# Lower parts of the first feed-forward weights by an adding DMA, and matmuls grouped by width

## The chip, the cores and the metric

The kernel runs on one core of one Trainium2 chip. The metric is the device time of one execution in microseconds (us). Before the change it is 2393.61 us, the median of 3 runs (2393.53 to 2394.68).

## The reference

Two transformer blocks, one after the other, on 256 tokens of width 2048 in float32. The first block has a modulated norm, a mixer of dilated attention and a gated recurrence, and a feed-forward part; the second has stick-breaking attention and a feed-forward part. The change lies in the two feed-forward parts, which are alike:

```python
# first block
h2 = rms_norm(x, norm2_w[l]) * (1.0 + scale2) + shift2
ff = jnp.square(jax.nn.relu(h2.astype(dt) @ w_ff1[l])) @ w_ff2[l]
x = x + (gate2 * ff.astype(jnp.float32)).astype(dt)
# second block
def squared_relu_mlp(h, w_in, w_out):
    return jnp.square(jax.nn.relu(h @ w_in)) @ w_out
h = h + squared_relu_mlp(rms_norm_2(h, norm_mlp_g[i]), mlp_w_in[i], mlp_w_out[i])
```

`w_ff1` and `mlp_w_in` are 2048 x 8192, `w_ff2` and `mlp_w_out` 8192 x 2048. All weights are read once, from HBM.

## The kernel before

TensorE works on a rounded 32-bit type (`F32R`) here, so each float32 operand is held as two: `hi`, its rounded value, and `lo`, what rounding left out. A product is the sum of three matmuls: hi by hi, hi by lo, lo by hi.

Weights come in chunks of 256 rows by 512 columns (512 KB). `chunk` (L222) makes one: SP's queue loads `raw`, ACT copies it to `hi` (L230), DVE subtracts `hi` from `raw` into `lo` (L231). There are 7 buffers of `raw` (RAW), shared with the loads of the modulation weights `w_ada`, and 4 each of `hi` and `lo` (HL). Both operations have a raised priority (AHEAD), so the scheduler, which fixes the order of every engine when the program is built, puts them well ahead of the matmuls that use the chunk.

Three functions consume chunks. `gemm` (L237) has the weights as the moving operand, 512 wide, 12 matmuls for a chunk. `gemm_t` (L250) has them as the stationary operand, with 24 matmuls of 256 columns. `gemm_wide` (L265), the one the change touches, also has the weights stationary, and for each of its 8 pairs in a chunk issues one matmul of 512 columns with `hi` (the upper and lower parts of the activations side by side, L275) and one of 256 columns with `lo` (the upper part alone, L276). Its four accumulators are two banks of `psA` (`acc`) and two of `psB` (`ps`).

`ffn` (L847) is called once for each block. For each quarter of the hidden width it runs four blocks of 8 chunks into `hT` (a wide phase: 32 chunks of `w_ff1` or `mlp_w_in`), then 32 chunks of `gemm` with the second weights. Only in the first quarter of the first call are two of the four blocks done by `gemm_t`. So `gemm_wide` runs 30 times, on 240 chunks, in seven phases of 32 chunks and one of 16. After each block ACT copies four pieces out of the accumulators (L866), DVE adds the other halves (L867) and squares (L868), ACT rounds the result (L869) and DVE subtracts (L870).

During the first `ffn`, `tick` also issues one load of `w_ada` (512 KB) for every four chunks (L916), until these 32 loads are done. POOL does a few memsets only, and issues no DMA.

Of the kernel before, what the change touches and what calls it, by code (L numbers as in the profile page):

```python
# [10 lines left out]
F32 = mybir.dt.float32  # L11
# [3 lines left out]
AF = mybir.ActivationFunctionType  # L15
ALU = mybir.AluOpType
AX = mybir.AxisListType

P = 128
T = 256  # L20
D = 2048
NK = D // P
# [3 lines left out]
KC = 2  # L26
# [14 lines left out]
def kernel(ctx: ExitStack, tc: tile.TileContext, I: dict, out: bass.AP, dbg=None):  # L41
    nc = tc.nc
    V, S, G, TE = nc.vector, nc.scalar, nc.gpsimd, nc.tensor
# [156 lines left out]
    def step(queue):  # L200
        while queue:
            try:
                next(queue[0])
                return
            except StopIteration:
                queue.pop(0)
# [4 lines left out]
    def tick():  # L211
        for name, queue in (("ada", ada_queue), ("side", side_queue)):
            due[name] += rate[name]
            while due[name] >= 1.0:
                due[name] -= 1.0
                step(queue)
# [2 lines left out]
        while queue:  # L219
            step(queue)  # L220

    def chunk(w, r0, c0):  # L222
        raw = wp.tile([P, KC, 512], F32, tag="raw", name="raw", bufs=RAW)
        nc.sync.dma_start(
            out=raw, in_=w[r0 : r0 + KC * P, c0 : c0 + 512].rearrange("(j p) n -> p j n", p=P)
        )
        hi = wp.tile([P, KC, 512], F32R, tag="hi", name="hi")
        lo = wp.tile([P, KC, 512], F32R, tag="lo", name="lo")
        with tc.high_priority(offset=AHEAD):
            S.copy(hi, raw)  # L230
            V.tensor_tensor(lo, raw, hi.bitcast(F32), ALU.subtract)  # L231
        return hi, lo

    def banks2():
        return [psA.tile([P, 512], F32, tag="acc", name="acc") for _ in range(2)]

    def gemm(xh, xl, both, w, r0, c0, accs, kr=(0, NK), first=True, last=True):  # L237

        for k0 in range(kr[0], kr[1], KC):
            hi, lo = chunk(w, r0 + k0 * P, c0)  # L240
            for t in range(2):
                for j in range(KC):
                    k = k0 + j
                    a, b = xh[:, k, t * P : (t + 1) * P], xl[:, k, t * P : (t + 1) * P]
                    TE.matmul(accs[t], a, hi[:, j, :], start=first and k == kr[0], stop=False)  # L245
                    TE.matmul(accs[t], a, lo[:, j, :], start=False, stop=False)  # L246
                    TE.matmul(accs[t], b, hi[:, j, :], start=False, stop=last and k == kr[1] - 1)  # L247
            tick()

    def gemm_t(xh, xl, both, w, r0, c0, accs, kr=(0, NK), first=True, last=True):  # L250

        for k0 in range(kr[0], kr[1], KC):
            hi, lo = chunk(w, r0 + k0 * P, c0)
            for m in range(4):
                o = accs[m // 2][:, (m % 2) * T : (m % 2 + 1) * T]
                for j in range(KC):
                    k = k0 + j
                    a, b = hi[:, j, m * P : (m + 1) * P], lo[:, j, m * P : (m + 1) * P]

                    TE.matmul(o, a, xh[:, k, :], start=first and k == kr[0] and m % 2 == 0, stop=False, skip_group_check=True)  # L260
                    TE.matmul(o, a, xl[:, k, :], start=False, stop=False, skip_group_check=True)  # L261
                    TE.matmul(o, b, xh[:, k, :], start=False, stop=last and k == kr[1] - 1, skip_group_check=True)  # L262
            tick()

    def gemm_wide(xh, xl, both, w, r0, c0, accs):  # L265

        for k0 in range(0, NK, KC):
            hi, lo = chunk(w, r0 + k0 * P, c0)  # L270
            for m in range(4):
                for j in range(KC):
                    k = k0 + j
                    a, b = hi[:, j, m * P : (m + 1) * P], lo[:, j, m * P : (m + 1) * P]
                    TE.matmul(accs[m], a, both[:, k, :, :], start=k == 0, stop=False, skip_group_check=True)  # L275
                    TE.matmul(accs[m][:, T : 2 * T], b, xh[:, k, :], start=False, stop=k == NK - 1,  # L276
                              skip_group_check=True)
            tick()

    def transposes(dst, src):  # L280
# [202 lines left out]
    for g, kr in enumerate(GROUPS[:-1]):  # L483
        while len(ready) <= g:
            ada_tick()
        for f, c0 in early:
            accs = banks2()
# [18 lines left out]
    ang, m, n, tmp, na = (sp.tile([P, 32], F32, tag="rope", name="rope", bufs=5) for _ in range(5))  # L506
# [314 lines left out]
    for b in range(4):  # L821
        accs = banks2()
# [24 lines left out]
    def ffn(xT, w1, w2, done, halfway=None):  # L847
        facc = None
        for c in range(4):
# [7 lines left out]
            for b in range(4):  # L857
                if b < len(pend):
                    accs = pend[b]
                    gemm_t(*xT, w1, 0, b * 512, accs, kr=(8, 16), first=False)  # L860
                else:
                    accs = banks2() + [bank(), bank()]
                    gemm_wide(*xT, w1, 0, c * D + b * 512, accs)
                    r = big().rearrange("p (a b) -> p a b", a=4)
                    for m in range(4):
                        S.copy(r[:, m, :], accs[m][:, T : 2 * T])  # L866
                        V.tensor_tensor(r[:, m, :], r[:, m, :], accs[m][:, 0:T], ALU.add)  # L867
                    V.scalar_tensor_tensor(r, r, 0.0, r, ALU.max, ALU.mult)  # L868
                    S.copy(hT[0][:, 4 * b : 4 * b + 4, :], r)  # L869
                    V.tensor_tensor(hT[1][:, 4 * b : 4 * b + 4, :], r, hT[0][:, 4 * b : 4 * b + 4, :].bitcast(F32),  # L870
                                    ALU.subtract)
                    continue
                for i in range(2):
                    k = b * 4 + i * 2
                    r = big()[:, 0:512].rearrange("p (a b) -> p a b", a=2)
                    S.activation(r, accs[i].rearrange("p (a b) -> p a b", a=2), AF.Relu)
                    V.tensor_tensor(r, r, r, ALU.mult)
                    S.copy(hT[0][:, k : k + 2, :], r)
                    V.tensor_tensor(hT[1][:, k : k + 2, :], r, hT[0][:, k : k + 2, :].bitcast(F32), ALU.subtract)
# [110 lines left out]
    for b in range(4):  # L990
# [4 lines left out]
        if b in pend:  # L995
            accs = pend.pop(b)
            gemm(*oT, wo, 0, b * 512, accs, kr=(12, 16), first=False)
        else:
            accs = banks2()
# [83 lines left out]
```

## Time and profile before

| | |
|---|---|
| median of 3 runs | 2393.61 us |
| the profiled execution | 2398.15 us, of which the span from first to last instruction is 2396.4 us |
| TensorE busy | 97% of the span, mean granted clock 0.993 |
| VectorE, ScalarE, GpSimd busy | 65%, 49%, 0% |
| HBM read | 514.95 MB, mean 216 GB/s over the span |

PE is TensorE, PEld its weight loads, DVE VectorE, ACT ScalarE, POOL GpSimd, SP SyncE, which here issues nearly all loads. Matmuls are pipelined: the duration of one (0.28 or 0.40 us) is longer than the distance from its start to the next one's start, and it is this distance that counts. A few per cent of the matmul records can be missing from a trace. Idle time of an engine that bounds nothing costs nothing. A group's releaser, after the arrow, is what ended most of its waiting.

### The profile page before, as it was taken

The numbers are of one execution on the slowest core, as the hardware profiler recorded it, in microseconds if no ns is written. First come the engines' busy times: TensorE is split into PE (matmuls) and PEld (weight loads), VectorE is DVE, ScalarE is ACT, GpSimd is POOL, SyncE is SP. The second block draws the span as 40 slices with busy tenths as digits, with TensorE's granted clock in tenths as the row PEclk, the third lists the DMA queues.
The fourth block names the chain that finished last, engine by engine and source line by source line (L and its number), as shares of the span: only waits on it lengthen the run. The fifth ranks groups of instructions, "written<-read, shape, count | busy, mean of one in ns | idle before, by whom it ended". The sixth has DMA issues, their size and how long they took to land.

```text
span 2396.4 us, 31309 instructions
## 1 busy us (share of the span) xinstructions
PE 2334.1 (97%) x11951; PEld 1972.5 (82%) x11951; DVE 1554.5 (65%) x1871; ACT 1174.2 (49%) x1749; POOL 5.9 (0%) x10
## 2 busy tenths in 40 slices
PE   5999999998999999999999999999999999999999
PEld 4887888877988888888888888888888888888887
DVE  7899888878665665555566555565654554555564
ACT  4535575644444444444445566655544443443442
POOL 0000000000000000000000000000000000000000
PEclk9999999998999999999999999999999999999999
DMA  9998787887777776666656555555666666666663
GB/s 347 333 318 272 260 293 248 271 294 274 229 239 235 231 237 211 186 192 189 188 185 186 178 169 163 162 171 177 187 191 194 187 190 194 185 191 194 186 196 129
DMA packets 252312, 519.10 MB, mean 217 GB/s; under 512 B 16689, under 2 KB 17278, under 8 KB 251906
## 3 DMA queue, kind: packets, MB, share of 16 engines
q1 hardware_dynamic: 252010, 517.03, 67.6%
q8 instruction: 93, 1.52, 0.3%
q14 instruction: 57, 0.47, 0.1%
q10 hardware_dynamic: 152, 0.08, 0.0%
HBM read 514.95 MB, written 2.10 MB: 216 GB/s over the span
## 4 chain that ended last, share of the span: by engine, by line
PE 88%; DVE 6%; issue 3%; DMA 2%; ACT 1%; SPq 0%; DVEq 0%; ACTq 0%
PE acc L246 16%; PE acc L247 16%; PE acc L245 16%; PE ps L275 9%; PE acc L275 9%; PE acc L276 5%; PE ps L276 5%; DVE lo L231 2%; PE acc L262 2%; PE ps L281 2%; PE acc L261 2%; PE acc L260 2%; DMA raw<-in_w_ada_dram 1%; PE ps L641 1%; DVE w L447 1%
## 5 line engine op out<-in xcount | busy, mean ns | idle before, releaser
L231 DVE TENSOR_TENSOR lo<-raw,hi 128x1024 fp32r<-128x1024 f32 x784 | 958.5, 1223 | 740.4 <-ACT hi L230 738.3
L230 ACT CAST hi<-raw 128x1024 fp32r<-128x1024 f32 x784 | 823.3, 1052 | 1026.4 <-PE acc L247 576.2
L245 PE MATMUL acc<-hi,yT 128*128 128x512 f32 x1280 | 501.0, 391 | 0.0
L246 PE MATMUL acc<-lo,yT 128*128 128x512 f32 x1280 | 499.7, 390 | 0.0
L247 PE MATMUL acc<-hi,yT 128*128 128x512 f32 x1280 | 499.5, 390 | 0.0
L275 PE MATMUL acc<-xT,hi 128*128 128x512 f32 x960 | 350.1, 399 | 0.0
L275 PE MATMUL ps<-xT,hi 128*128 128x512 f32 x960 | 349.2, 398 | 0.0
L246 PE MATMUL acc<-lo,xT 128*128 128x512 f32 x704 | 279.6, 397 | 4.2 <-DVE lo L231 3.6
L247 PEld LDWEIGHTS acc<-hi,yT 128*128 128x128 f32 x1280 | 241.0, 188 | 50.1
L245 PEld LDWEIGHTS acc<-hi,yT 128*128 128x128 f32 x1280 | 240.9, 188 | 49.7
L246 PEld LDWEIGHTS acc<-lo,yT 128*128 128x128 f32 x1280 | 241.0, 188 | 49.2
L247 PE MATMUL acc<-hi,xT 128*128 128x512 f32 x704 | 276.7, 393 | 0.0
L245 PE MATMUL acc<-hi,xT 128*128 128x512 f32 x704 | 276.0, 398 | 0.0
L276 PE MATMUL acc<-xT,lo 128*128 128x256 f32 x960 | 269.6, 281 | 0.0
L276 PE MATMUL ps<-xT,lo 128*128 128x256 f32 x960 | 269.5, 281 | 0.0
L275 PEld LDWEIGHTS acc<-xT,hi 128*128 128x128 f32 x960 | 180.3, 188 | 44.4 <-ACT hi L230 0.5
L275 PEld LDWEIGHTS ps<-xT,hi 128*128 128x128 f32 x960 | 180.3, 188 | 44.3
L140 DVE SCALAR_TENSOR_TENSOR ada<-raw,csil,ada 128x1024 f32<-128x1024 f32 x124 | 158.6, 1280 | 43.2 <-DMA raw<-in_w_ada_dram 42.6
L276 PEld LDWEIGHTS acc<-xT,lo 128*128 128x128 f32 x960 | 181.4, 189 | 0.8 <-issue 0.5
L276 PEld LDWEIGHTS ps<-xT,lo 128*128 128x128 f32 x960 | 181.4, 189 | 0.0
L246 PEld LDWEIGHTS acc<-lo,xT 128*128 128x128 f32 x704 | 132.9, 189 | 36.9 <-DVE lo L231 10.8
L247 PEld LDWEIGHTS acc<-hi,xT 128*128 128x128 f32 x704 | 132.8, 189 | 26.8 <-issue 0.2
(226 smaller groups left out, 1935.2 us busy)
## 6 DMA issues: line engine op xcount, KB each, us to landing
raw<-in_w_ff_dram SPq DMA_DIRECT2D x256, 512.0 KB, 4.0
raw<-in_w_ada_dram SPq DMA_DIRECT2D x160, 512.0 KB, 4.8
raw<-in_mlp_w_in_dram SPq DMA_DIRECT2D x128, 512.0 KB, 3.7
raw<-in_mlp_w_out_dram SPq DMA_DIRECT2D x128, 512.0 KB, 3.7
raw<-in_w_in_dram SPq DMA_DIRECT2D x112, 512.0 KB, 5.8
raw<-in_sb_w_qkv_dram SPq DMA_DIRECT2D x96, 512.0 KB, 3.9
ada<-in_w_ada_dram SPq DMA_DIRECT2D x32, 512.0 KB
raw<-in_w_out_dram SPq DMA_DIRECT2D x32, 512.0 KB, 5.5
```

Source lines behind the costliest of these rows:

```text
L140: V.scalar_tensor_tensor(acc, w, csil[:, k : k + 1], acc, ALU.mult, ALU.add)
L230: S.copy(hi, raw)
L231: V.tensor_tensor(lo, raw, hi.bitcast(F32), ALU.subtract)
L245: TE.matmul(accs[t], a, hi[:, j, :], start=first and k == kr[0], stop=False)
L246: TE.matmul(accs[t], a, lo[:, j, :], start=False, stop=False)
L247: TE.matmul(accs[t], b, hi[:, j, :], start=False, stop=last and k == kr[1] - 1)
L260: TE.matmul(o, a, xh[:, k, :], start=first and k == kr[0] and m % 2 == 0, stop=False, skip_group_check=True)
L261: TE.matmul(o, a, xl[:, k, :], start=False, stop=False, skip_group_check=True)
L262: TE.matmul(o, b, xh[:, k, :], start=False, stop=last and k == kr[1] - 1, skip_group_check=True)
L275: TE.matmul(accs[m], a, both[:, k, :, :], start=k == 0, stop=False, skip_group_check=True)
L276: TE.matmul(accs[m][:, T : 2 * T], b, xh[:, k, :], start=False, stop=k == NK - 1, skip_group_check=True)
L281: TE.transpose(dst, src, ident)
```

## The change

In the chunks of `gemm_wide` alone, DVE's subtraction is taken out. ACT, which still makes `hi`, now also writes minus `raw`, rounded like `hi`, into `lo`, and POOL issues a DMA that reads the same 512 KB of weights from HBM a second time and adds them onto `lo`. The sum is again `raw` minus `hi`. In `gemm_wide` the eight 512-wide matmuls of a chunk now come first and the eight 256-wide ones after them.

```diff
@@ -219,16 +219,20 @@
         while queue:
             step(queue)
 
-    def chunk(w, r0, c0):
+    def chunk(w, r0, c0, by_dma=False):
+        src = w[r0 : r0 + KC * P, c0 : c0 + 512].rearrange("(j p) n -> p j n", p=P)
         raw = wp.tile([P, KC, 512], F32, tag="raw", name="raw", bufs=RAW)
-        nc.sync.dma_start(
-            out=raw, in_=w[r0 : r0 + KC * P, c0 : c0 + 512].rearrange("(j p) n -> p j n", p=P)
-        )
+        nc.sync.dma_start(out=raw, in_=src)
         hi = wp.tile([P, KC, 512], F32R, tag="hi", name="hi")
         lo = wp.tile([P, KC, 512], F32R, tag="lo", name="lo")
         with tc.high_priority(offset=AHEAD):
             S.copy(hi, raw)
-            V.tensor_tensor(lo, raw, hi.bitcast(F32), ALU.subtract)
+            if by_dma:
+                S.activation(lo, raw, AF.Copy, scale=-1.0)
+                G.dma_start(out=lo, in_=src, accum_op=ALU.add)
+            else:
+                V.tensor_tensor(lo, raw, hi.bitcast(F32), ALU.subtract)
         return hi, lo
 
     def banks2():
@@ -267,14 +271,17 @@
 
 
         for k0 in range(0, NK, KC):
-            hi, lo = chunk(w, r0 + k0 * P, c0)
+            hi, lo = chunk(w, r0 + k0 * P, c0, by_dma=True)
             for m in range(4):
                 for j in range(KC):
                     k = k0 + j
-                    a, b = hi[:, j, m * P : (m + 1) * P], lo[:, j, m * P : (m + 1) * P]
-                    TE.matmul(accs[m], a, both[:, k, :, :], start=k == 0, stop=False, skip_group_check=True)
-                    TE.matmul(accs[m][:, T : 2 * T], b, xh[:, k, :], start=False, stop=k == NK - 1,
+                    TE.matmul(accs[m], hi[:, j, m * P : (m + 1) * P], both[:, k, :, :], start=k == 0, stop=False,
                               skip_group_check=True)
+            for m in range(4):
+                for j in range(KC):
+                    k = k0 + j
+                    TE.matmul(accs[m][:, T : 2 * T], lo[:, j, m * P : (m + 1) * P], xh[:, k, :], start=False,
+                              stop=k == NK - 1, skip_group_check=True)
             tick()
 
     def transposes(dst, src):
```

In PE's program, at the seam of two chunks of the first wide blocks, the rows before are these. `Activation` is the semaphore of ACT (`hi` is ready), `DVE` that of DVE (`lo` is ready).

```order
L275 MATMUL ps<-xT,hi 128x512
L276 MATMUL ps<-xT,lo 128x256
L275 MATMUL acc<-xT,hi 128x512 [waits Activation_49]
L276 MATMUL acc<-xT,lo 128x256 [waits DVE_49]
L275 MATMUL acc<-xT,hi 128x512
L276 MATMUL acc<-xT,lo 128x256
```

After the change one whole chunk there reads as follows. `DMASW1` is the semaphore of a DMA that POOL issued; the matmuls with `hi` are now at L278 and those with `lo` at L283.

```order
L278 MATMUL acc<-xT,hi 128x512 [waits Activation_49]
L278 MATMUL acc<-xT,hi 128x512 x3
L278 MATMUL ps<-xT,hi 128x512 x4
L283 MATMUL acc<-xT,lo 128x256 [waits DMASW1_49]
L283 MATMUL acc<-xT,lo 128x256 x3
L283 MATMUL ps<-xT,lo 128x256 x4
```

The eight wide matmuls have moved ahead of the eight narrow ones, and the first narrow one waits for a DMA where it waited for DVE.

In ACT's program, at the end of a wide block in the first `ffn`, the rows before are these (`hi<-raw` is the rounding of a chunk, L866 and L869 are the copies of the finished block).

```order
L230 CAST hi<-raw 128x1024 [waits DMAHW3_49,DVE_49,PE_49]
L230 CAST hi<-raw 128x1024 [waits DMAHW4_49,DVE_49,PE_49]
L230 CAST hi<-raw 128x1024 [waits DMAHW6_49,DVE_49,PE_49]
L866 COPY w<-acc 128x256 [waits PE_49] x2
L866 COPY w<-ps 128x256 [waits PE_49]
L230 CAST hi<-raw 128x1024 [waits DMAHW7_49,DVE_49,PE_49]
L866 COPY w<-ps 128x256 [waits PE_49]
L230 CAST hi<-raw 128x1024 [waits DMAHW0_49,DVE_49,PE_49]
L869 CAST yT<-w 128x4x256 [waits DVE_49]
```

After the change that place reads as follows (L229 is the rounding, L232 the new pass, L873 and L876 the copies).

```order
L229 CAST hi<-raw 128x1024 [waits DMAHW1_49,PE_49,Activation_49]
L232 ACTIVATE lo<-raw 128x1024 [waits DMASW4_49,PE_49]
L229 CAST hi<-raw 128x1024 [waits DMAHW2_49,PE_49,Activation_49]
L232 ACTIVATE lo<-raw 128x1024 [waits DMASW5_49,PE_49]
L229 CAST hi<-raw 128x1024 [waits DMAHW4_49,PE_49,Activation_49]
L232 ACTIVATE lo<-raw 128x1024 [waits DMASW6_49,PE_49]
L229 CAST hi<-raw 128x1024 [waits DMAHW5_49,PE_49,Activation_49]
L873 COPY w<-acc 128x256 [waits PE_49]
L232 ACTIVATE lo<-raw 128x1024 [waits DMASW7_49,PE_49]
L873 COPY w<-acc 128x256
L873 COPY w<-ps 128x256 x2
L229 CAST hi<-raw 128x1024 [waits DMAHW6_49,PE_49,Activation_49]
L232 ACTIVATE lo<-raw 128x1024 [waits DMASW0_49,PE_49]
L876 CAST yT<-w 128x4x256 [waits DVE_49]
```

Each rounding is now followed by a pass that writes `lo`; that pass waits for PE to have done with the buffer's last use and for an earlier DMA of POOL. POOL's program, which held memsets alone, now ends in 240 DMAs, one per such pass, each behind a wait for ACT.

## Rows read from the trace of the kernel before

**Rows 1.** The page's head: busy time and share of each engine.
```profile
PE 2334.1 (97%) x11951; PEld 1972.5 (82%) x11951; DVE 1554.5 (65%) x1871; ACT 1174.2 (49%) x1749; POOL 5.9 (0%) x10
```

**Rows 2.** The page's chain that ended last, shares by engine.
```profile
PE 88%; DVE 6%; issue 3%; DMA 2%; ACT 1%; SPq 0%; DVEq 0%; ACTq 0%
```

**Rows 3.** The page's costliest groups: name, count | busy, mean ns | idle.
```profile
L231 DVE TENSOR_TENSOR lo<-raw,hi 128x1024 fp32r<-128x1024 f32 x784 | 958.5, 1223 | 740.4 <-ACT hi L230 738.3
L230 ACT CAST hi<-raw 128x1024 fp32r<-128x1024 f32 x784 | 823.3, 1052 | 1026.4 <-PE acc L247 576.2
...
L275 PE MATMUL acc<-xT,hi 128*128 128x512 f32 x960 | 350.1, 399 | 0.0
...
L276 PE MATMUL acc<-xT,lo 128*128 128x256 f32 x960 | 269.6, 281 | 0.0
```

**Rows 4.** Timeline of PE in a wide block: start, duration, instruction.
```profile
1879.87 0.40 PE L275 MATMUL acc<-xT,hi 128*128 128x512 f32 x1
...
1880.23 0.40 PE L275 MATMUL ps<-xT,hi 128*128 128x512 f32 x1
1880.46 0.28 PE L276 MATMUL ps<-xT,lo 128*128 128x256 f32 x1
...
1880.93 0.40 PE L275 MATMUL ps<-xT,hi 128*128 128x512 f32 x1
```

**Rows 5.** Timeline of PE in the second product: 512-wide matmuls.
```profile
2002.77 0.39 PE L246 MATMUL acc<-lo,yT 128*128 128x512 f32 x1
2003.00 0.39 PE L247 MATMUL acc<-hi,yT 128*128 128x512 f32 x1
```

**Rows 6.** Timeline of PE in the transposed product: 256-wide matmuls.
```profile
583.09 0.28 PE L262 MATMUL acc<-xT,lo 128*128 128x256 f32 x1
583.21 0.28 PE L260 MATMUL acc<-xT,hi 128*128 128x256 f32 x1
```

**Rows 7.** Windows: stretch, engines' busy time, clock, DMA share, GB/s.
```profile
0.00:100.00 100.00, 70.27 (x413) 61.88 (x414) 79.43 (x131) 52.78 (x91) 0.20 (x4) 1.00 0.96 345
500.00:600.00 100.00, 88.76 (x497) 78.39 (x496) 84.42 (x107) 42.31 (x64) 1.91 (x2) 0.90 0.83 284
763.00:853.00 90.00, 90.00 (x492) 76.94 (x491) 62.76 (x64) 43.03 (x53) 0.00 (x0) 1.00 0.73 225
1859.00:1950.00 91.00, 91.00 (x516) 78.87 (x516) 51.21 (x53) 42.55 (x52) 0.00 (x0) 1.00 0.64 186
```

**Rows 8.** DMA in the first 100 us, 40 slices; last number: landing.
```profile
DMA  2999999999995299999999999998889999999889
GB/s 43 299 406 428 419 384 388 385 389 386 387 387 171 22 349 401 386 390 383 388 384 385 389 383 388 387 384 285 279 288 388 338 381 372 354 329 369 311 238 361
...
raw<-in_w_ada_dram SPq DMA_DIRECT2D x20, 512.0 KB, 10.1
```

**Rows 9.** DMA queue and issue rows of the whole page.
```profile
q1 hardware_dynamic: 252010, 517.03, 67.6%
...
raw<-in_mlp_w_in_dram SPq DMA_DIRECT2D x128, 512.0 KB, 3.7
```

**Rows 10.** ACT's groups between 1880 and 1960 us, four blocks' ends.
```profile
L230 ACT CAST hi<-raw 128x1024 fp32r<-128x1024 f32 x28 | 29.4, 1051 | 37.9 <-PE ps L275 34.0 <-PE acc L247 3.9
L869 ACT CAST yT<-w 128x1024 fp32r<-128x1024 f32 x4 | 4.2, 1054 | 0.2
L866 ACT COPY w<-acc 128x256 f32<-128x256 f32 x8 | 3.0, 369 | 0.9 <-PE acc L276 0.9
```

**Rows 11.** Waits in a wide phase: total us, times, longest.
```profile
ACT hi L230 <- PE ps L275: 39.3, 28, 1.7
DVE lo L231 <- ACT hi L230: 30.7, 24, 1.5
```

**Rows 12.** Timeline of PE after a gap: the same 256-wide matmuls.
```profile
594.48 0.41 PE L260 MATMUL acc<-xT,hi 128*128 128x256 f32 x1
594.69 0.41 PE L261 MATMUL acc<-xT,hi 128*128 128x256 f32 x1
```

## The prediction

> **What bounds the kernel now.** I read the page's busy shares first, then its chain, then the costliest groups, and then the stages by windows. TensorE is busy 97% of the span and VectorE 65% [rows 1]; the chain is PE for 88% of the span [rows 2]. So the time taken from VectorE is not time taken from the kernel: its subtraction sits idle 740 us in total, nearly all of it waiting for ACT's rounding [rows 3], and that rounding in turn waits in a wide phase for TensorE to give a buffer back [rows 11]. Everything in a wide phase waits for TensorE. In such a phase PE has no gap (91 of 91 us busy, clock 1.00), and the DMA engines are busy 0.64 at 186 GB/s; in the first feed-forward part, where loads of w_ada run beside, 0.73 at 225 GB/s [rows 7]. The transfers have room, but not for a second copy of all weights without more ado. That is where the change must be weighed.
>
> **What grouping gives.** In the timeline of a wide block three pairs of a wide and a narrow matmul take 1880.93 - 1879.87 = 1.06 us, 0.353 each; the wide one takes 0.23 of it [rows 4]. Where 512-wide matmuls follow each other they start every 0.227 us (2003.00 after 2002.77 gives 0.23; over four starts it is 0.2275) [rows 5], and 256-wide ones alone every 0.12 us [rows 6]. Grouped, a pair would cost 0.347, 0.006 less. A chunk has 8 pairs: 2.83 us before, 2.78 after. With 240 chunks the gain is at most 240 x 0.048 = 11.5 us, and only where TensorE still sets the pace. That is all the change can win on TensorE; its count of matmuls and columns is the same.
>
> **What leaves VectorE, and what ACT gets.** 240 subtractions of 1.22 us (293 us) go from VectorE [rows 3]. I count nothing for them, since VectorE waited there. ACT gets 240 more passes over 128x1024. The trace has no such pass with a factor of -1; the nearest row is the rounding, 1.05 us, of the same shape and types [rows 10]. ACT's load for a chunk becomes 1.05 + 1.05, plus an eighth of a block's end (four copies of 0.37 and one rounding of 1.05 [rows 10], 2.53 / 8 = 0.32): 2.42 us of the 2.78 that TensorE needs. That fits with 0.36 to spare. If it did not, ACT would be next in line; as a bound, at a pass of 1.5 us it would be 2.87, or 0.09 x 240 = 22 us. A buffer of `raw` is now given back by ACT and not by VectorE, at about the same point. SP's loads stand behind that. The copies of a finished block stand behind at most one pass more in ACT's order, and there are two sets of accumulators, so I give them nothing.
>
> **The adding DMA.** This is the term that decides. For each of the 240 chunks the DMA engines carry a second 512 KB from HBM, and to add it they must also fetch the 512 KB that already stand in `lo`. The trace of before has no adding transfer and none issued by POOL, so its price is bounded. The rate of a full queue is in the first 100 us: in the slices between 12 and 30 us, with the engines at 0.9 or more, 384 to 389 GB/s, I take 387 [rows 8]. So 524,288 bytes cost 1.355 us when the engines are full.
> - Low end: adding costs what a plain load costs, 1.355 us. With the load, 2.71 us a chunk, just below TensorE's 2.78. All of it would be hidden, and the grouping's 11.5 us would remain: 2393.6 - 11.5 = 2382.
> - Middle: the two sources pass through the engines one after the other, 2.71 us. With the load, 4.06 us a chunk, and TensorE waits.
> - High end: not the rate but the delay of each transfer. There are 4 buffers of `lo`; between two uses of one stand a rounding and a pass of ACT (2.10), the transfer, and the eight narrow matmuls (0.96). A plain load lands after 3.7 us at ordinary load [rows 9] and after 10.1 with the queue full [rows 8]. At 10.1 a chunk takes (2.10 + 10.1 + 0.96) / 4 = 3.3 us, +113 us over 240 chunks; at twice that, for two streams, 5.8 us, and +715 us (2393.6 + 715 = 3109).
>
> I take the middle: the sources are two by the nature of the operation, and the nearest row for each is the full rate. What the buffers soften: when a wide phase begins, the transfers for its first 4 chunks can already have been made in the phase before; the lead of 7 loads of `raw` is the same at both ends. So a phase of 32 chunks carries 32 x 1.355 + 28 x 2.71 = 43.4 + 75.9 = 119.2 us, against 32 x 2.83 = 90.6 us of TensorE before: +28.6. Seven such phases give 200 us. The phase of 16 chunks gives 16 x 1.355 + 12 x 2.71 = 54.2 against 45.3: +9. In the first two wide phases the loads of w_ada come on top: the one from 763 to 853 us moves 225 GB/s where 186 would do for the weights [rows 7], 39 x 90 us = 3.5 MB or 6.7 loads; the half phase has about half of that; some 10 loads x 1.355 = 14 us. Sum: 200 + 9 + 14 = 223 us. The grouping's gain is not taken off, as the DMA engines set the pace there. Against the profiled execution: 2398.15 + 223 = 2621; the median of the runs is 4.5 us below that execution, so 2617. I give 2620.
>
> On the other side stands the Trainium skill, page "DMA: Bandwidth & Descriptors", section "Where 436 GB/s comes from": SBUF's DMA ports carry 435 GB/s together. Two plain streams in 2.78 us are 377 GB/s and would fit below that; by this figure the change would be hidden and the time 2382. The trace's own full queue reaches 387 with plain loads alone (a single slice 428 [rows 8]), which is no proof for adding ones. The same page's section "SWDGE vs HWDGE vs iDMA" has accumulating done through GpSimd alone, and its fit for DMAs issued there, 2.0 us plus the bytes at 436 GB/s, gives an estimated 3.2 us for 512 KB; no run here shows it yet, and if these DMAs came strictly one behind the other it would be 2394 + 240 x 0.37 = 2480.
>
> **The rivals.**
> 1. *All hidden, grouping pays* (2382, 2377 to 2389). For it: two plain streams need 2.71 us, less than 2.78, and the engines showed 428 GB/s in one slice. Against it: it leaves 3% of room, w_ada's loads come on top in two phases, and adding must fetch `lo` too. It holds only if an adding transfer costs no more than 1.42 us of the engines.
> 2. *Nearly hidden* (2389 to 2480): adding costs between one and one and a half plain loads; at 1.5 (2.03) a phase carries 43.4 + 56.9 = 100 us, +9.7, which with the half phase and w_ada is some 80 us, or 2475.
> 3. *The ring of four buffers or POOL sets the pace* (2760 to 3110): slower than forecast. POOL takes the DMAs one by one, and PE stands at the first narrow matmul of the chunk with all later ones behind it; PE's queue is in order, so ACT, waiting for that buffer, stops, and SP's loads behind ACT stop too. From a landing of about 13.2 us on, this passes the 4.06 of the forecast, (2.10 + 13.2 + 0.96) / 4.
> 4. *The clock falls.* Waiting 1.3 of each 4.06 us, TensorE might drop to its lower level, as it did in the stretch at 0.90 mean clock [rows 7], where after a gap narrow matmuls came every 0.21 us [rows 12] instead of 0.12 (1.2 GHz for 2.4). A chunk would take 5.56 us: 240 x 2.73 = 655 us, 3050. Against it: in the first 100 us PE was busy 70% and had 1.00 all through [rows 7]; the forecast has it busy 68%.
>
> **How the numbers follow.** A change of less than 0.2% (5 us) counts as none. The forecast (2480 to 2760) gets 0.50, rival 1 0.09, rival 2 0.19 (a quarter of that within 5 us of now), rivals 3 and 4 together 0.22. So faster 0.09, same 0.05, slower 0.86. The range 2400 to 2950 leaves out rival 1 and the near end of rival 2, and the far part of rivals 3 and 4, some 0.2 in all.
>
> **What would show it.** Right: in the wide phases the DMA share is near 1 and PE below 75%, its idle time ahead of the first narrow matmul with a DMA as releaser; outside of them the distances are as before; wide matmuls start every 0.227 us and narrow ones every 0.12. The bytes read grow by 240 x 0.524 = 126 MB. Wrong: PE still at 100% in those phases (rival 1), or the DMA engines well below full while PE waits (rival 3), or a granted clock below 1 there (rival 4).

## The result: slower by 12%, the DMA engines set the pace

The changed kernel takes 2687.0 us (2682.7 to 2688.2, 4 runs) against 2394.1 for the kernel before, run beside it: a ratio of 1.1213, 95% interval 1.1197 to 1.1230. That is 293 us more. The forecast was 2620, in a range of 2400 to 2950. The bytes read from HBM grew as forecast, by 126 MB (514.95 to 640.78).

The page of the changed kernel, busy shares and the chain:

```profile
PE 2394.6 (89%) x11951; PEld 1959.2 (73%) x11951; DVE 1265.6 (47%) x1631; ACT 1411.1 (53%) x1989; POOL 294.9 (11%) x250
...
PE 42%; DMA 29%; issue 19%; DVE 6%; ACT 3%; POOL 1%; SPq 0%; DVEq 0%; POOLq 0%; ACTq 0%
DMA lo<-in_mlp_w_in_dram 15%; DMA lo<-in_w_ff_dram 11%; PE acc L250 10%; PE acc L251 10%; PE acc L249 10%; DVE lo L235 2%; PE acc L266 2%; PE ps L288 2%; PE acc L265 1%; PE acc L283 1%; PE acc L264 1%; ACT lo L232 1%; DMA raw<-in_w_ada_dram 1%; PE ps L283 1%; ACT hi L229 1%
```

TensorE is busy 89% of a longer span, where it had 97% [rows 1], and only 42% of the chain is PE's, where it was 88% [rows 2]. The adding DMAs have taken 26% of the chain: 15% for the second block's weights in the row above, 11% for the first's. The groups that answer to [rows 3] and [rows 10]:

```profile
L235 DVE TENSOR_TENSOR lo<-raw,hi 128x1024 fp32r<-128x1024 f32 x544 | 662.3, 1223 | 522.4 <-ACT hi L229 391.6
...
L232 ACT ACTIVATE lo<-raw 128x1024 fp32r<-128x1024 f32 x240 | 254.8, 1062 | 205.9 <-PE ps L283 182.1
...
L233 POOL DMA_DIRECT2D lo<-in_mlp_w_in_dram x128 | 154.1, 1204 | 1102.2 <-ACT lo L232 1064.7
```

VectorE lost 296 us of subtractions and the kernel won nothing by it. ACT's new pass takes 1.06 us, as the rounding does [rows 10]. POOL spends 1.20 us on each of its DMAs. Two stretches of wide phases, the first with loads of w_ada beside, the second without (columns as in [rows 7]):

```profile
780.00:900.00 120.00, 87.81 (x445) 69.18 (x444) 21.19 (x26) 60.15 (x70) 31.29 (x26) 0.94 1.09 271
2060.00:2160.00 100.00, 76.17 (x401) 59.20 (x400) 14.32 (x20) 56.58 (x63) 27.70 (x23) 1.00 1.10 262
```

Where PE was busy 91 of 91 us with the DMA engines at 0.64 and 186 GB/s [rows 7], it is now busy 76 of 100 with the engines at 1.10. (The forecast's sign was below 75; in the first stretch it is 73%.) The share is the time that packets took, summed over queues, so above 1 it says that packets overlap; by itself it does not say that the engines are full, as a run below shows 1.15 where PE never waits. At 262 GB/s, two times 524,288 bytes take 4.00 us; the forecast had 4.06. PE's granted clock was 1.00 in the second stretch, and 0.94 on average in the first. What PE waited for, from the first wide phase to the last:

```profile
PE acc L283 <- DMA lo<-in_mlp_w_in_dram: 119.0, 125, 1.9
PE acc L283 <- DMA lo<-in_w_ff_dram: 104.7, 95, 5.9
```

Those 224 us, in 220 waits of about a microsecond, all lie ahead of the first narrow matmul of a chunk. (PE's busy time also spans the tails of matmuls, so that the waits in this view are shorter than the time lost.) The DMA view of that second stretch:

```profile
GB/s 262 260 264 260 262 261 261 262 261 261 264 261 261 261 262 262 261 261 261 262 262 261 263 262 261 261 263 261 262 262 261 262 262 261 264 261 262 262 261 262
...
q0 software_dynamic: 6770, 13.05, 70.4%
q1 hardware_dynamic: 6773, 13.05, 39.4%
...
lo<-in_mlp_w_in_dram POOLq DMA_DIRECT2D x23, 512.0 KB, 13.4
```

The rate is flat at 260 to 264 GB/s in every slice of 2.5 us. A queue that was not there before, q0, carries POOL's transfers. An adding DMA lands 13.4 us after its issue, where a load took 3.7 [rows 9].

The phases, from the first to the last start of a matmul of `gemm_wide` in the trace of PE, in us (each matmul counted by itself, also where the timeline merges four into a row, x4):

| | half phase | 2nd | 3rd | 4th | 5th to 8th | sum |
|---|---|---|---|---|---|---|
| before | 45.1 | 92.0 | 92.0 | 90.3 | 89.7 to 90.3 | 680 |
| changed | 63.8 | 134.5 | 129.2 | 127.2 | 127.3 to 128.2 | 966 |

The two profiled executions (2398.2 and 2688.2 us) are 290 us apart. Of these, 286 lie inside the phases of `gemm_wide`, and 8.5 in the two stretches after the first two phases (87.2 us before; 92.5 and 90.4 now), beside which loads of w_ada run; the stretch ahead of the first phase is 4.5 us shorter.

### The profile page after: what moved, and what is told of

It is laid out like the page before. It is cut to its first block, busy times and chain, and to the rows that moved or that the text cites. A ratio compares the mean times of both kernels' runs of the same rounds, so it can differ in the third digit from the quotient of the medians.

```text
span 2686.4 us, 31943 instructions
## 1 busy us (share of the span) xinstructions
PE 2394.6 (89%) x11951; PEld 1959.2 (73%) x11951; DVE 1265.6 (47%) x1631; ACT 1411.1 (53%) x1989; POOL 294.9 (11%) x250
## 3 DMA queue, kind: packets, MB, share of 16 engines
q0 software_dynamic: 65280, 125.84, 25.3%
HBM read 640.78 MB, written 2.10 MB: 239 GB/s over the span
## 4 chain that ended last, share of the span: by engine, by line
PE 42%; DMA 29%; issue 19%; DVE 6%; ACT 3%; POOL 1%; SPq 0%; DVEq 0%; POOLq 0%; ACTq 0%
DMA lo<-in_mlp_w_in_dram 15%; DMA lo<-in_w_ff_dram 11%; PE acc L250 10%; PE acc L251 10%; PE acc L249 10%; DVE lo L235 2%; PE acc L266 2%; PE ps L288 2%; PE acc L265 1%; PE acc L283 1%; PE acc L264 1%; ACT lo L232 1%; DMA raw<-in_w_ada_dram 1%; PE ps L283 1%; ACT hi L229 1%
## 5 line engine op out<-in xcount | busy, mean ns | idle before, releaser
L229 ACT CAST hi<-raw 128x1024 fp32r<-128x1024 f32 x784 | 821.1, 1049 | 846.4 <-PE acc L251 528.0
L235 DVE TENSOR_TENSOR lo<-raw,hi 128x1024 fp32r<-128x1024 f32 x544 | 662.3, 1223 | 522.4 <-ACT hi L229 391.6
L250 PE MATMUL acc<-lo,yT 128*128 128x512 f32 x1280 | 499.6, 390 | 5.9 <-DVE lo L235 5.9
L283 PE MATMUL acc<-xT,lo 128*128 128x256 f32 x960 | 178.4, 308 | 224.0 <-DMA lo<-in_mlp_w_in_dram 119.0
L283 PEld LDWEIGHTS acc<-xT,lo 128*128 128x128 f32 x960 | 130.9, 191 | 321.2 <-DMA lo<-in_mlp_w_in_dram 172.4
L232 ACT ACTIVATE lo<-raw 128x1024 fp32r<-128x1024 f32 x240 | 254.8, 1062 | 205.9 <-PE ps L283 182.1
L250 PE MATMUL acc<-lo,xT 128*128 128x512 f32 x704 | 280.2, 398 | 4.2 <-DVE lo L235 3.9
L250 PEld LDWEIGHTS acc<-lo,yT 128*128 128x128 f32 x1280 | 240.8, 188 | 56.4 <-DVE lo L235 7.3
L251 PEld LDWEIGHTS acc<-hi,yT 128*128 128x128 f32 x1280 | 240.7, 188 | 49.9
L233 POOL DMA_DIRECT2D lo<-in_mlp_w_in_dram x128 | 154.1, 1204 | 1102.2 <-ACT lo L232 1064.7
L278 PE MATMUL acc<-xT,hi 128*128 128x512 f32 x960 | 265.9, 399 | 0.0
L874 DVE TENSOR_TENSOR w<-w,acc 128x256 f32<-128x256 f32 x60 | 24.1, 418 | 501.3 <-ACT w L873 501.3
L278 PE MATMUL ps<-xT,hi 128*128 128x512 f32 x960 | 260.1, 393 | 0.0
L278 PEld LDWEIGHTS ps<-xT,hi 128*128 128x128 f32 x960 | 182.4, 190 | 41.1
L233 POOL DMA_DIRECT2D lo<-in_w_ff_dram x112 | 135.0, 1205 | 644.8 <-ACT lo L232 610.8
L278 PEld LDWEIGHTS acc<-xT,hi 128*128 128x128 f32 x960 | 166.5, 191 | 23.1 <-issue 0.7
## 6 DMA issues: line engine op xcount, KB each, us to landing
lo<-in_mlp_w_in_dram POOLq DMA_DIRECT2D x128, 512.0 KB, 13.4
lo<-in_w_ff_dram POOLq DMA_DIRECT2D x112, 512.0 KB, 13.4
```

The source lines that it names most:

```text
L232: S.activation(lo, raw, AF.Copy, scale=-1.0)
L233: G.dma_start(out=lo, in_=src, accum_op=ALU.add)
L278: TE.matmul(accs[m], hi[:, j, m * P : (m + 1) * P], both[:, k, :, :], start=k == 0, stop=False, skip_group_check=True)
L283: TE.matmul(accs[m][:, T : 2 * T], lo[:, j, m * P : (m + 1) * P], xh[:, k, :], start=False, stop=k == NK - 1, skip_group_check=True)
```

## The experiments

Two theories had to be told apart, since the trace of the changed kernel fits both. The chain there runs through one buffer of `lo` again and again:

```profile
2083.70 0.74 PE acc L283 x4
2084.44 0.49 PE ps L283 x4
...
2084.95 1.07 ACT lo L232
2086.02 0.29 issue
2086.31 13.36 DMA lo<-in_mlp_w_in_dram
```

Narrow matmuls (1.23 us), ACT's pass (1.07), 0.29, then 13.4 of the transfer, and the buffer is used again four chunks on: 15.95 / 4 = 4.0 us a chunk. That is also what full DMA engines give. Either the engines are full, and the 13.4 us are queueing (the theory); or an adding DMA has a long delay of its own, and the ring of four buffers sets the pace (the rival). And within the theory: which part of an adding transfer costs?

### Grouping alone

```diff
-            hi, lo = chunk(w, r0 + k0 * P, c0, by_dma=True)
+            hi, lo = chunk(w, r0 + k0 * P, c0)
```

> Grouping alone: the eight 512-wide matmuls first, then the eight 256-wide ones, lo by VectorE's subtraction as before, no adding DMA. Theory (the DMA engines set the pace of the changed kernel): 240 chunks x 0.048 us = 11.5 us less than before, 2382 (2378 to 2390), wide matmuls every 0.227 us, narrow ones every 0.12, a wide phase 89 us, DMA share 0.65. Rival (grouping itself costs, since 256-wide matmuls in a row lay their weight loads bare): narrow ones start 0.15 us or more apart, a pair 0.377, 2394 + 240 x 8 x 0.024 = 2440.

Measured: 2387.2 us (8 runs) against 2393.7, ratio 0.9973, interval 0.9962 to 0.9984. A wide phase takes 89.2 us where it took 90.3 (91.0 where it took 92.0); the eight together 674 against 680. A stretch of a phase, and PE's rows around a chunk (the last two rows are the starts of two chunks):

```profile
2030.00:2110.00 80.00, 80.00 (x461) 70.44 (x460) 45.88 (x47) 36.47 (x44) 0.00 (x0) 1.00 0.61 190
```

```profile
2086.07 0.64 PE L283 MATMUL ps<-xT,lo 128*128 128x256 f32 x4
2086.55 1.09 PE L278 MATMUL acc<-xT,hi 128*128 128x512 f32 x4
...
2089.34 1.09 PE L278 MATMUL acc<-xT,hi 128*128 128x512 f32 x4
```

PE is busy throughout. A chunk takes 2.79 us, where 2.83 were measured before and 2.78 worked out for now. So grouping gives about half of the bound of 11.5 us: 6 us inside the phases, and 4 to 9 us in the whole. The rival is out: narrow matmuls in a row start every 0.12 us and cost nothing extra.

### The adding DMA alone

```diff
                     k = k0 + j
-                    TE.matmul(accs[m], hi[:, j, m * P : (m + 1) * P], both[:, k, :, :], start=k == 0, stop=False,
+                    a, b = hi[:, j, m * P : (m + 1) * P], lo[:, j, m * P : (m + 1) * P]
+                    TE.matmul(accs[m], a, both[:, k, :, :], start=k == 0, stop=False, skip_group_check=True)
+                    TE.matmul(accs[m][:, T : 2 * T], b, xh[:, k, :], start=False, stop=k == NK - 1,
                               skip_group_check=True)
-            for m in range(4):
-                for j in range(KC):
-                    k = k0 + j
-                    TE.matmul(accs[m][:, T : 2 * T], lo[:, j, m * P : (m + 1) * P], xh[:, k, :], start=False,
-                              stop=k == NK - 1, skip_group_check=True)
             tick()
```

> The adding DMA alone, with wide and narrow matmuls alternating as before. Theory (DMA engines full at 4.0 us a chunk): the wide phases stay at 127 us, time as the changed kernel's 2687 within 10 us, since TensorE does not set the pace there. Rival (the ring of four lo buffers with a fixed delay of 13.4 us sets it): the first narrow matmul, and with it the whole chunk, now waits from the chunk's start, the buffer is held for 2.83 us instead of 0.96, so a chunk takes (2.4 + 13.4 + 2.8) / 4 = 4.65 us, 2687 + 240 x 0.6 = 2830.

Measured: 2697.6 us, ratio 1.1274 (1.1256 to 1.1291), 0.6 us beyond the theory's 10. A phase takes 129.4 us. A stretch of one, and the landing on the page:

```profile
2060.00:2140.00 80.00, 61.32 (x320) 48.82 (x320) 11.18 (x17) 46.02 (x55) 24.09 (x20) 1.00 1.10 263
...
lo<-in_mlp_w_in_dram POOLq DMA_DIRECT2D x128, 512.0 KB, 10.9
```

263 GB/s, as before. Although a chunk now holds its buffer of `lo` for 2.8 us and not for 1.2, the rate is the same, and the landing has become shorter, 10.9 us for 13.4. This speaks for full engines: the delay gives way, the rate does not. Beside the adding DMA, too, the grouped kernel is the faster one, by some 10 us; by what way, when TensorE waits anyhow, no run tells.

### A plain copy in place of the adding one

```diff
-                G.dma_start(out=lo, in_=src, accum_op=ALU.add)
+                G.dma_start(out=lo, in_=src)
```

> The changed kernel with POOL's DMA copying the weights into lo instead of adding them (lo is then the whole weight instead of its lower part: the output is not the reference's). Same bytes from HBM, same count of DMAs, same waits, same POOL work; the fetch of lo's old contents is gone. Theory (two streams through the DMA engines make the price): a chunk needs 2.71 us of the engines, hidden or nearly, 2385 to 2420, PE 97% busy or more in the wide phases. Rival A (HBM's second read is the price): as the changed kernel, 2687. Rival B (POOL's descriptor work or the delay of any DMA from POOL is the price): as the changed kernel or within 30 us of it.

Measured: 2406.8 us, ratio 1.0048 (1.0032 to 1.0065). Its queue and POOL's row on the page, and a wide phase:

```profile
q0 software_dynamic: 65280, 125.84, 17.4%
...
L233 POOL DMA_DIRECT2D lo<-in_mlp_w_in_dram x128 | 91.3, 713 | 1011.7 <-ACT lo L232 975.7
```

```profile
2050.00:2125.00 75.00, 75.00 (x431) 65.99 (x430) 13.12 (x19) 58.48 (x69) 18.54 (x26) 1.00 1.15 373
```

The same 126 MB, from the same place, by the same queue, at 373 GB/s, and PE never waits in this stretch; the phases from the fourth on take 89.2 to 90.1 us, as with grouping alone. What is left of a loss lies in the second phase (100.9 us, against 91.0 with grouping alone), beside w_ada. So the second read of the weights from HBM by itself is all but hidden, and the price belongs to the adding. POOL, too, is quicker with a plain copy, 0.71 us against 1.20, so its work is not held equal here; the last run below holds it.

### Adding from SBUF

```diff
-                G.dma_start(out=lo, in_=src, accum_op=ALU.add)
+                G.dma_start(out=lo, in_=raw, accum_op=ALU.add)
```

> The changed kernel with the adding DMA reading raw in SBUF instead of the weights in HBM; the result is the same, and HBM is read once. Theory (engines busy with two sources and one load): 4.06 us a chunk still, 2687 within 40 us; a little more, as raw is held until the transfer has landed. Rival (HBM's second read is the price): HBM traffic is as before, a chunk 2.78 us, 2385 to 2420.

Measured: 2622.8 us, ratio 1.0958 (1.0937 to 1.0979); a phase from the fourth on takes 116.5 to 118.8 us. Its queue, a stretch of a phase, and what ACT waited for in the phases and between:

```profile
q0 software_dynamic: 34560, 125.84, 24.3%
```

```profile
2020.00:2100.00 80.00, 66.19 (x335) 51.63 (x335) 11.06 (x18) 45.90 (x56) 17.24 (x20) 0.96 1.06 275
```

```profile
ACT hi L229 <- DMA raw<-in_w_ff_dram: 140.3, 54, 7.9
ACT hi L229 <- DMA raw<-in_mlp_w_in_dram: 136.1, 47, 5.1
```

Neither side: HBM's second read is gone and 229 of the 293 us remain. So HBM is not the price; but the time fell by 64 us, more than the 40 that the theory allowed. The page counts 34,560 packets here and 65,280 in the changed kernel, so the packets are twice as long, as a row of `raw` in SBUF is contiguous over both halves. Another thing differs: ACT's rounding now waits 276 us for loads (the two rows together), where it waits 19 us in the changed kernel, so the loads have become the later of the two streams. The next two runs compare source and packet length.

### Splitting the adding DMA, from HBM and from SBUF

The second of the two kernels has `raw[:, j, :]` as the source.

```diff
-                G.dma_start(out=lo, in_=src, accum_op=ALU.add)
+                for j in range(KC):
+                    G.dma_start(out=lo[:, j, :], in_=src[:, j, :], accum_op=ALU.add)
```

> The changed kernel with each adding DMA split into two, one for each 128 rows; the packets are the same 2 KB, POOL issues twice as many. Theory (DMA engines full): 2687 within 20 us. Rival (POOL's issuing, 1.2 us each, stands in the way): slower by up to 240 x 1.2 = 288 us.

> The adding DMA with raw in SBUF as its source, split into two as in the run before, so that its packets are 2 KB and not 4 KB (34,560 packets in the unsplit one, 65,280 in the changed kernel). If the 64 us that the source in SBUF saved came from the missing second read of HBM: 2622 within 15. If they came from the packets' size: 2687 within 20.

Measured from HBM: 2698.2 us, ratio 1.1273 (1.1250 to 1.1295). From SBUF: 2666.0 us, ratio 1.1138 (1.1116 to 1.1161), in neither of the two bands, with this queue:

```profile
q0 software_dynamic: 69120, 125.86, 25.9%
```

Twice as many DMAs cost 11 us, not 288: POOL's issuing does not stand in the way. With packets of 2 KB on both sides, the source in SBUF is 32 us ahead of the one in HBM; unsplit, with packets of 4 KB, it is 43 us further, of which 11 may be what splitting costs by the pair from HBM. So of the 64 us about half goes with the source and half with the packet length, and neither removes the loss. How longer packets help is not shown: with them the loads fall behind, which the split run does not have (27 us of waits for them).

### Three buffers of lo

```diff
-        lo = wp.tile([P, KC, 512], F32R, tag="lo", name="lo")
+        lo = wp.tile([P, KC, 512], F32R, tag="lo", name="lo", bufs=3)
```

> The changed kernel with 3 buffers of lo instead of 4, nothing else. Theory (DMA engines full, 4.0 us a chunk; the 13.4 us to landing are queueing, so they shrink with fewer transfers in flight): landing falls to some 9.5 us, a chunk stays near 4.0, 2687 to 2720. Rival (the ring of buffers with a fixed delay): a turn of 1.23 of PE + 1.07 of ACT + 0.29 + 13.7 of the transfer = 16.3 us, now for 3 chunks, 5.43 each, 2687 + 240 x 1.4 = 3030.

Measured: 2708.0 us, ratio 1.1314 (1.1291 to 1.1336). Landing, and a stretch of a phase:

```profile
lo<-in_mlp_w_in_dram POOLq DMA_DIRECT2D x25, 512.0 KB, 9.4
```

```profile
2260.00:2340.00 80.00, 62.77 (x320) 49.01 (x318) 9.49 (x15) 47.23 (x52) 23.77 (x20) 1.00 1.06 258
```

The landing fell from 13.4 to 9.4 us, by one chunk's 4.0, and the rate stayed (258 GB/s). A fixed delay would have given 3030. The ring is not what limits; the transfers wait for one another.

### Adding in every second chunk

```diff
-            hi, lo = chunk(w, r0 + k0 * P, c0, by_dma=True)
+            hi, lo = chunk(w, r0 + k0 * P, c0, by_dma=(k0 // KC) % 2 == 1)
```

> The adding DMA in every second chunk only; VectorE's subtraction in the others. Theory (DMA engines): a full chunk takes 4.0 us of them, a load alone 1.355, so two chunks take 5.36, 2.68 each, just below TensorE's 2.78: nearly hidden, 2385 to 2410, where w_ada runs beside a little over. Rival (ring with a fixed delay): every turn of four buffers still holds a transfer of 13.7 us, 4.07 us a chunk, 2680.

Measured: 2418.0 us, ratio 1.0109 (1.0092 to 1.0126), 8 us above the band.

```profile
2260.00:2340.00 80.00, 79.86 (x435) 68.63 (x434) 35.30 (x38) 46.03 (x55) 12.03 (x10) 1.00 0.94 257
```

Half of the adding costs 24 us where all of it costs 293: a threshold, as full engines give, and no ring. The phases from the fourth on take 90.2 to 91.8 us; the excess lies in the half phase (49.9), the second (102.4) and the third (95.0). Beside the first two run loads of w_ada; the third's excess is not explained.

### Adding without the loads

`once` holds one chunk, loaded at the start. The lines that make it, and `RAW = 6` in place of 7, are left out here.

```diff
-        raw = wp.tile([P, KC, 512], F32, tag="raw", name="raw", bufs=RAW)
-        nc.sync.dma_start(out=raw, in_=src)
+        if by_dma:
+            raw = once[0]
+        else:
+            raw = wp.tile([P, KC, 512], F32, tag="raw", name="raw", bufs=RAW)
+            nc.sync.dma_start(out=raw, in_=src)
```

> The changed kernel without the loads of raw in gemm_wide: hi and minus raw are made from one chunk that is loaded once (6 buffers of raw, for the room), while the 240 adding DMAs stay (the output is not the reference's). This takes the load's share of the DMA engines away and leaves the adding alone. Theory (prices add up on the engines: 4.0 = 1.355 + 2.65): 2.65 us a chunk, below TensorE's 2.78, so hidden, 2375 to 2410, DMA share near 0.95 to 1. Rival (the adding transfers are held up by something of their own, as their order on POOL or their delay, and the load is hidden beside them): a chunk stays well above 2.78, 2550 to 2690.

Measured: 2401.7 us, ratio 1.0044 (1.0032 to 1.0055). Queue and landing on the page, a stretch of a late phase, and two of the second phase:

```profile
q0 software_dynamic: 65280, 125.84, 30.5%
...
lo<-in_mlp_w_in_dram POOLq DMA_DIRECT2D x128, 512.0 KB, 6.1
```

```profile
2230.00:2310.00 80.00, 80.00 (x458) 70.25 (x457) 18.00 (x26) 59.33 (x73) 30.10 (x25) 1.00 1.05 192
```

```profile
756.00:769.00 13.00, 9.26 (x49) 7.12 (x48) 1.28 (x1) 6.62 (x7) 4.10 (x4) 1.00 1.10 262
772.00:782.00 10.00, 8.72 (x45) 6.65 (x45) 0.00 (x0) 5.59 (x7) 3.30 (x3) 1.00 1.13 207
```

The same adding DMAs, one per 2.79 us, and PE does not wait in the late phases; from the fourth on they take 89.2 to 90.1 us. (The share is 1.05, a little above the 0.95 to 1 that was expected.) The second phase shows the sum of the two streams at work within one run. At its start loads that SP issued ahead still run beside the adding: 262 GB/s together, PE waits, and from 757 to 770 us an adding DMA lands every 4.0 us, as in the changed kernel. When these loads end, at about 771, the transfers still queued land every 2.55 us (773.90, 776.45, 779.00, 781.54), at 207 GB/s, and PE's waits are over. So an adding DMA alone takes 2.55 us and a load 1.355, 3.9 in sum, and the two together take 4.0. Take away either the adding (the plain copy) or the loads (this run) and the loss is gone; it is the sum of both that does not fit into TensorE's 2.79.

## Why the prediction was right, and where its sum was short

*What bounds the kernel.* Right: time taken from VectorE was worth nothing, and its removal cost nothing.

*Grouping.* Right in place, about twice too large: distances of 0.23 and 0.12 us, but 2.79 us a chunk and not 2.78, and 6 us in the phases when done alone, for a bound of 11.5. The first four wide matmuls of a chunk start 0.23 us apart and not 0.2275. The forecast counted nothing for it beside the adding DMA; there the kernel takes 10 us more without it.

*ACT.* Right: 1.06 us a pass, and it waits for PE, not PE for it.

*The adding DMA's price.* Right in size, 4.00 us a chunk for 4.06. The forecast took the operation's two sources as the reason. That the price belongs to the adding is shown (plain copy; no loads; one read of HBM); that it comes from fetching `lo` is not: no run takes the fetch away and leaves the adding. With a load at 1.355 us, what the adding takes is 4.00 - 1.355 = 2.65; the run without loads shows 2.55 when nothing runs beside it, for the forecast's 2.71. How close the number came is in part luck: by the forecast's reason the run from SBUF should have kept 4.06 us a chunk, as its expectation said, and its phases give 117 / 32 = 3.66, so the price also hangs on source and packet length.

*The ceiling and the estimate of 3.2 us.* Two plain streams are hidden at 373 GB/s in the plain copy, while the adding with the loads did not pass a flat 262. The Trainium skill, page "DMA: Bandwidth & Descriptors", section "Where 436 GB/s comes from", gives a ceiling of 435 GB/s; both rates are below it, and it did not decide here. When it stood alone, POOL's adding DMA went out every 2.79 us without a wait of PE and landed after 6.1 us, so these DMAs overlap; strictly one behind the other they are not. By the fit that the same page of the Trainium skill gives in its section "Anatomy of one DMA — SWDGE (gpsimd) path", the forecast's estimate for one of this size was 3.2 us; the measured landing is nearly twice that.

*Rivals 1 and 2* failed by the price. *Rival 3* (ring or POOL) is refuted by three buffers and by the split; that the landing came to 13.4 us, just where the ring alone would give 4.06 too, is why the trace of the changed kernel could not tell them apart. *Rival 4*: the granted clock was 0.97 in the half phase, 0.95 in the second and 0.99 to 1.00 in the others, and these take the full 4.00 us a chunk; not the cause.

*The sum.* It came to 223 us, the time to 293. The step that failed in size is the head start: "when a wide phase begins, the transfers for its first 4 chunks can already have been made in the phase before". POOL's DMAs, one pass of ACT, and PE's matmuls around the start of the sixth phase:

```profile
2030.06 1.20 POOL L233 DMA_DIRECT2D lo<-in_mlp_w_in_dram  x1 [93.57 <-ACT lo L232]
2032.78 1.20 POOL L233 DMA_DIRECT2D lo<-in_mlp_w_in_dram  x1 [1.52 <-ACT lo L232]
2035.50 1.20 POOL L233 DMA_DIRECT2D lo<-in_mlp_w_in_dram  x1 [1.51 <-ACT lo L232]
2038.22 1.20 POOL L233 DMA_DIRECT2D lo<-in_mlp_w_in_dram  x1 [1.52 <-ACT lo L232]
2042.32 1.20 POOL L233 DMA_DIRECT2D lo<-in_mlp_w_in_dram  x1 [2.90 <-ACT lo L232]
2046.26 1.20 POOL L233 DMA_DIRECT2D lo<-in_mlp_w_in_dram  x1 [2.74 <-ACT lo L232]
```

```profile
2031.42 1.06 ACT L232 ACTIVATE lo<-raw 128x1024 fp32r<-128x1024 f32 x1 [0.72 <-PE acc L250]
```

```profile
2036.88 1.07 PE L278 MATMUL acc<-xT,hi 128*128 128x512 f32 x4
2037.79 1.07 PE L278 MATMUL ps<-xT,hi 128*128 128x512 f32 x4
2039.70 0.74 PE L283 MATMUL acc<-xT,lo 128*128 128x256 f32 x4 [0.84 <-DMA lo<-in_mlp_w_in_dram]
2040.28 0.64 PE L283 MATMUL ps<-xT,lo 128*128 128x256 f32 x4
2040.76 1.09 PE L278 MATMUL acc<-xT,hi 128*128 128x512 f32 x4
```

The first adding DMA goes out at 2030.06, the phase begins at 2036.88, and the first narrow matmul waits until 2039.70, already 0.84 us of idle time, for just that transfer. The passes came one per 2.72 us, as the `gemm` before (L250 is its matmul with `lo`) gave its buffers of `lo` back, and from the phase's start on the transfers ran at the full 262 GB/s. So none of the four was ready, a phase of 32 chunks takes 32 x 4.00 = 128 us (127.2 to 128.2 measured from the fourth on), and 7 x (128 - 90.6) + (64 - 45.3) = 281 us, against the 286 found in the phases. The forecast's 28 adding transfers a phase in place of 32 were worth 4 x 2.71 = 10.8 us in each of eight phases, 87 in all; the price of 4.00 in place of 4.06 takes 240 x 0.06 = 14 back, and 73 is the shortfall of 70 but for 3. The loads of w_ada were put at 14 us. The second phase grew by 42.5 us where the later ones grew by some 37.5, so by 5.0 more, the third by no more than these; with the 8.5 after the first two phases that makes 13.5. That all of it is due to w_ada is not shown: the granted clock was below 1 there at times.

## What to carry to other kernels

Before work is moved from an idle engine to the DMA engines, price a stage by its transfers, not the whole kernel by its mean: here 512 KB in 2.8 us left room for one more plain stream and not for an adding one. An adding transfer can cost much more than its bytes: here 2.55 us, nearly two plain ones of 1.355. Buffers in a ring give a head start only if the stage before gives them back early enough; when a chain of waits shows a long transfer, change the number in flight: if the landing shrinks and the pace stays, the rate limits and not the delay.

## What the runs showed of the hardware that was not expected

- An adding DMA of 512 KB in packets of 2 KB holds POOL for 1.20 us, a plain copy of the same shape for 0.71; from SBUF in packets of 4 KB the adding one holds it for 0.86.
- With adding DMAs and loads together the engines carried 262 GB/s, with adding from SBUF 275 in the stretch shown, with plain copies and loads 373, with adding alone 207.
- From SBUF, 240 adding transfers of 512 KB in packets of 4 KB took 43 us less than 480 halves in packets of 2 KB (2622.8 and 2666.0); 11 us of that may be the split's, by the pair from HBM.
